# Hybrid Hawk/S5 trunk: four plain pairs of w_up for both halves of the tokens, and a norm plan that makes the plain operands first

## The chip, the cores and the metric

The kernel runs on one core of a Trainium2 chip. Its engines are TensorE (PE; its weight loads are shown apart as PEld), VectorE (DVE), ScalarE (ACT), GpSimd (POOL) and SyncE (SP), which here issues all DMA. Each takes its instructions in the order in which they were recorded. The metric is device time in microseconds of one execution; less is better.

## The reference, cut to what matters

One layer on 1024 prompt tokens and 8 sequences of 4 sample tokens, 1056 tokens of 1024 features. The two groups share weights and differ in state and in the conditioning vectors. All of it is float32.

```python
u = x * (1 + sc1) + sh1
z = u @ w_in + b_in                      # LRU, gate, S5 and merge inputs
...                                      # RG-LRU branch, S5 branch with weight GLU
gl = gelu(ys) @ w_s5_glu
br_b = gl[..., :D_MODEL] * sigmoid(gl[..., D_MODEL:])
mixed = (sigmoid(m_a) * br_a + sigmoid(m_b) * br_b) @ w_out
x = layer_norm(ALPHA * x + g1 * mixed, ln1_g, ln1_b)
u2 = x * (1 + sc2) + sh2
hf = u2 @ w_ffn_up                       # 1024 -> 2 * 2816
f = (silu(hf[..., :D_FF]) * hf[..., D_FF:]) @ w_ffn_down
x = layer_norm(ALPHA * x + g2 * f, ln2_g, ln2_b)
```

## The kernel before

Tokens lie along the free axis, features on the 128 partitions. Every product is made of three matmuls: each operand is split into a high part (a rounded copy, made by ACT) and a low part (the rest, made by a subtraction on DVE or POOL, `lo_part`, which the profile shows as line 117), and high x high, high x low and low x high are summed in one PSUM bank. A weight tile is 128 outputs by 8 k tiles of 128; `WTile.split` makes its two parts in two halves of four k tiles each, ACT first, then DVE for w_up and POOL for all other weights. `use_w` splits one tile ahead of the one in use; raw tiles are loaded up to three ahead into a ring of three.

From the second GLU pass on, the tokens are four quarters of 264, two *halves* (s = 0: quarters 0 and 1; s = 1: quarters 2 and 3). The stages in order:

1. `glu(0)`, `out_pass(0)`, `glu(1)`, `out_pass(1)`: GLU products and output products of each half. The output products feed the first layer norm's sums.
2. The first norm of a half and the modulated operand `u2` of the up product are not one loop. `norm_plan` lists their operations with an engine, a cost and what each reads and writes; `Plan.emit` places them by a greedy schedule on ticks, and `tick()`, called once for each 24-matmul product, records those that are due. The plan of half 0 is recorded among the products of `glu(1)`, the plan of half 1 among the first up products.
3. The up product, 22 pairs j of weight tiles: tile j (the silu side) and tile 22 + j. The *plain way* costs 96 matmuls for a pair and a half: 2 tiles x 2 quarters x 8 k tiles x 3. The other way treats a pair as a 2x2 block product (k in two halves, quarters as columns) and uses the scheme with seven block products instead of eight: 7 x 4 k tiles x 3 = 84 matmuls, but it needs seven combinations of the weights (`prep`: subtractions on DVE, a copy on ACT, a low part) and eight operands of the tokens (0 to 7, `oper` in `norm_plan`), of which 1, 4, 5 and 7 are the four blocks themselves (b11, b21, b22, b12) and 0, 2, 3 and 6 are differences of them. The plain way uses 1, 4, 5 and 7.
4. The down product over the 22 feature tiles in five pieces of k (`DOWN`), `residual` on DVE, then the second norm.

In the up product before: pairs 0 to 4 go the plain way for half 0 alone, while the operands of half 1 are being made. Then come 22 *units* (`UNITS`): pairs 0 to 4 for half 1 alone, pairs 5 to 21 for both halves. In a unit of one half the low part of five of the seven weight combinations is made by DVE, in a unit of two halves all by POOL (`prep`). Operand 7 exists for half 0 alone and only for the plain way; its place is later the fifth buffer of the ring of weight combinations. The evacuations of a unit (`up_evac`) are ACT copies and tanh, and DVE additions and multiplications, in a chain from product to product. `half_out` writes each finished pair and half to a DRAM tensor, `d_f`.

At the start of down, `residual_scale` (ACT, line 1600) scales the normalised tokens, which had been spilled to `d_x`, for the residual; for quarter 1 the eight tiles stand together just ahead of the first down tile, after a load of 1 MB from `d_x` that is issued in the last unit. Feature tiles are loaded back from `d_f` (`f_load`) among the first down tiles.

Names in the rows: `small_t` holds raw weights, norm buffers and evacuation buffers; `rear_t` the tokens of the four quarters (`M`) and, later, differences; `r_t` the operands and the features; `weights_t` split weights; `ps` PSUM. Line 1170 is every matmul of glu, out and up, 1656 of down; 1364 the modulation, 1430 an operand's high part, 1507 a weight combination's, 230 a weight tile's; 1175, 1185 the GLU evacuation's ACT steps; 1559 the plain way's tanh; 1578, 1584, 1588 a unit's ACT steps.

Of the kernel before, what the change touches and what calls it, by code (L numbers as in the profile page):

```python
# [18 lines left out]
FFT = 22  # L19
# [12 lines left out]
PLAIN = 5  # L32
UNITS = [(j, (1,)) for j in range(PLAIN)] + [(j, (0, 1)) for j in range(PLAIN, FFT)]
# [38 lines left out]
def tile_hawk_s5(ctx: ExitStack, tc: tile.TileContext, io):  # L72
# [197 lines left out]
    for j in range(PLAIN):  # L270
        for m in (j, FFT + j):
            queue("up", io["w_up"][m], m)
# [9 lines left out]
    for i, w in enumerate(seq):  # L282
# [6 lines left out]
        elif not w.plain:  # L289
            w.place = lambda z=1024 * (n_split % 2): (wb, z, z + 2048)  # L290
            n_split += w.key != ("in", 15)
# [1030 lines left out]
    class Plan:  # L1322
# [3 lines left out]
        def __init__(self, us, **share):  # L1326
            self.us, self.share, self.ops, self.wrote, self.read = us, share, [], {}, {}
# [11 lines left out]
        def emit(self, first):  # L1339
# [18 lines left out]
            return first + int(max(end.values()) / self.us) + 1  # L1358
# [14 lines left out]
    def norm_plan(plan, s, rr, tmp):  # L1373
# [31 lines left out]
        bufs = dict(zip(names, tmp))  # L1405
        for c in range(2):
            for op in (sub_, mul):
                for i in range(2):
                    for h in range(2):
                        p.add("V", 0.7, (f"sum{i}", f"r{i}")[op == mul:][:1], (f"x{i}{h}{c}",),  # L1410
                              lambda c=c, i=i, h=h, op=op: normal(c, i, h, op))
# [4 lines left out]
            def mod(i, h, name, c=c):  # L1416

                k = tuple(f"{n}{j}" for n in "tvz" for j in range(2))
                p.add("A", 0.9, (f"x{i}{h}{c}",), (name, *k), lambda: modulated(q0 + i, h, c, bufs[name]))
                if q0 + i == 3:  # L1420
                    p.add("V", 0.8, (f"x{i}{h}{c}",), (name,), lambda: modulated_samples(h, c, bufs[name]))

            def diff(out, x, y):
                p.add("V", 0.7, (x, y), (out,), lambda: tt(V, bufs[out], bufs[x], bufs[y], sub_))

            def oper(e, v, name, c=c):
                o, f = operand(v, s), operand(v, s, FT)
                x = bufs[name]
                p.add("A", 0.65, (name,), (f"o{v}{c}",),
                      lambda: A.activation(o[:, 0, 2 * c:2 * c + 2], x, AF.Copy))  # L1430
                eng, us = {"V": (V, 0.75), "P": (P, 1.35)}[e]
                p.add(e, us, (name, f"o{v}{c}"), (),
                      lambda: lo_part(eng, o[:, 1, 2 * c:2 * c + 2], x, f[:, 0, 2 * c:2 * c + 2]))


            mod(0, 0, "b11")
            mod(1, 0, "b12")
            oper("P", 1, "b11")
            mod(1, 1, "b22")
            if s == 0:  # L1440
                oper("P", 7, "b12")
            mod(0, 1, "b21")
            diff("b11", "b12", "b11")
            diff("b12", "b22", "b12")
            oper("V", 2, "b11")
            oper("P", 5, "b22")
            diff("b11", "b22", "b11")
            oper("P", 3, "b12")
            oper("V", 0, "b11")
            oper("V", 4, "b21")  # L1450
            diff("b21", "b21", "b11")
            oper("P", 6, "b21")
# [8 lines left out]
    tmp1 = tuple(M[0][:, 2 * i:2 * i + 2] for i in range(4))  # L1461
    rr1 = {2: B[:, 4], 3: B[:, 5]}

# [62 lines left out]
    assert plan.emit(2) <= 30  # L1526
# [18 lines left out]
    assert plan.emit(1) <= 4 * PLAIN  # L1545
    for j in range(PLAIN):
        ff = B[:, 2 * (j % 2):2 * (j % 2) + 2]
        for m in (j, FFT + j):
            w = use_w("up", m)
# [312 lines left out]
```

## Time and profile before

| | |
|---|---|
| median of three runs | 1853.21 us (1853.14 to 1854.78) |
| profiled execution's own time | 1857.63 us, span of the core 1855.8 us |
| PE busy | 1731.2 us (93%), 13344 matmuls |
| DVE, ACT, POOL busy | 1200.9, 727.5, 1009.6 us |
| first plan starts (sums of half 0) | 926.5 us |
| plain pairs start, end | 1077.9, 1139.9 us |
| one-half units end, two-half units end | 1222.1, 1568.0 us |

A row of the timeline has the start, the time to the end of the last of the merged instructions, engine, line and tiles; in brackets stands the idle time just before and what ended it. A row of the windows has start and end, length, busy time of each engine with its count of instructions, then TensorE's granted clock, the DMA engines' share and GB/s. A row of grouped instructions has busy time and mean ns of one. A busy PE is not a PE at its peak: matmuls overlap, so the time of a stretch by its count is the better measure.

### The profile page before, as it was taken

Reading aid. Unit: us, or ns where it says so; the run is one execution under the profiler, and the core shown is the slowest. Engines: PE = TensorE matmul, PEld = TensorE weight load, DVE = VectorE, ACT = ScalarE, POOL = GpSimd, SP = SyncE. Lnnn points to the kernel's source line nnn. Section 1 sums busy time; section 2 is a strip of 40 time slices with the busy share of each in tenths; the row PEclk is TensorE's granted clock in tenths of the full one; section 3 lists DMA queues with packets and bytes.
Section 4 is the critical chain, followed back from the end, with each engine's and each line's share of the span. In section 5 each row is a group of like instructions: output and inputs, shape, how many; then the busy total and the mean of one; then the engine's idle time right before and its main releaser. Section 6 shows DMA issues by size and latency. Waiting matters only on the chain. (4 is left out here: it accounts for less than half of the span.)

```text
span 1855.8 us, 33890 instructions
## 1 busy us (share of the span) xinstructions
PE 1731.2 (93%) x13344; PEld 1689.3 (91%) x13344; DVE 1200.9 (65%) x1998; ACT 727.5 (39%) x1465; POOL 1009.6 (54%) x829
## 2 busy tenths in 40 slices
PE   6899999999788799999998998799999999999996
PEld 5889889999788799999998997699999999999996
DVE  6889999738878843322776588755545554543587
ACT  4433333335564543222354354334433333111234
POOL 3466657435666642345667723367677775322654
PEclk9999999999989899999999999999999999999998
DMA  9335544441111149675344333224223325932202
GB/s 346 103 102 148 154 137 136 141 133 44 60 52 39 48 126 245 213 241 195 112 148 150 121 100 119 101 86 149 93 93 122 110 93 196 381 125 78 80 31 65
DMA packets 118927, 241.98 MB, mean 130 GB/s; under 512 B 23152, under 2 KB 62320, under 8 KB 115696
## 3 DMA queue, kind: packets, MB, share of 16 engines
q1 hardware_dynamic: 118768, 239.81, 39.6%
q8 instruction: 105, 1.72, 0.4%
q14 instruction: 54, 0.44, 0.1%
HBM read 180.64 MB, written 54.97 MB: 127 GB/s over the span
## 5 line engine op out<-in xcount | busy, mean ns | idle before, releaser
L1170 PE MATMUL ps<-r_t,weights_t 128*128 128x264 f32 x5424 | 681.4, 286 | 26.9 <-DVE small_t L117 15.5
L1170 PEld LDWEIGHTS ps<-r_t,weights_t 128*128 128x128 f32 x5424 | 669.0, 189 | 34.7 <-DVE small_t L117 17.2
L117 POOL TENSOR_TENSOR weights_t<-small_t,weights_t 128x512 fp32r<-128x512 f32 (+3 forms) x292 | 368.7, 1278 | 422.9 <-ACT weights_t L230 333.3
L338 PE MATMUL ps<-r_t,weights_t 128*128 128x352 f32 x3384 | 572.4, 329 | 1.9 <-ACT weights_t L230 1.1
L338 PEld LDWEIGHTS ps<-r_t,weights_t 128*128 128x128 f32 x3384 | 554.6, 193 | 12.3 <-issue 7.9
L230 ACT ACTIVATE weights_t<-small_t 128x512 fp32r<-128x512 f32 (+3 forms) x274 | 144.5, 570 | 232.0 <-PE ps L1656 96.8
L126 DVE SCALAR_TENSOR_TENSOR rear_t<-ps,small_t,rear_t 128x264 f32<-128x264 f32 (+1 forms) x192 | 92.6, 482 | 124.1 <-PE ps L1656 102.5
L1656 PE MATMUL ps<-r_t,weights_t 128*128 128x264 f32 x1344 | 166.9, 286 | 4.9 <-ACT weights_t L230 4.9
L1656 PEld LDWEIGHTS ps<-r_t,weights_t 128*128 128x128 f32 x1344 | 165.7, 190 | 6.1 <-ACT weights_t L230 5.3
L117 DVE TENSOR_TENSOR small_t<-ps,small_t 128x264 f32<-128x264 f32 (+1 forms) x243 | 91.2, 382 | 105.9 <-ACT small_t L1578 75.8
L126 DVE SCALAR_TENSOR_TENSOR rear_t<-rear_t,ps 128x264 f32<-128x264 f32 (+1 forms) x75 | 33.6, 457 | 172.4 <-PE ps L1170 96.3
L117 DVE TENSOR_TENSOR s_t<-s_t 128x128 f32<-128x128 f32 (+3 forms) x200 | 134.4, 720 | 12.0 <-ACT s_t L747 6.3
L117 POOL TENSOR_TENSOR r_t<-rear_t,r_t 128x264 fp32r<-128x264 f32 (+2 forms) x76 | 95.2, 1256 | 74.2 <-ACT r_t L1185 28.5
L117 POOL TENSOR_TENSOR rear_t<-rear_t,small_t 128x264 f32<-128x264 f32 (+1 forms) x109 | 93.1, 876 | 66.0 <-ACT small_t L1233 44.3
L117 POOL TENSOR_TENSOR weights_t<-rear_t,weights_t 128x512 fp32r<-128x512 f32 x64 | 84.1, 1317 | 70.4 <-ACT weights_t L1507 68.0
L117 DVE TENSOR_TENSOR rear_t<-rear_t,small_t 128x32 f32<-128x32 f32 (+3 forms) x139 | 97.1, 707 | 38.7 <-POOL weights_t L117 28.4
L117 POOL TENSOR_TENSOR r_t<-small_t,r_t 128x528 fp32r<-128x528 f32 (+1 forms) x59 | 80.7, 1377 | 39.9 <-ACT r_t L209 26.3
L126 DVE SCALAR_TENSOR_TENSOR lru_t<-lru_t 128x1056 f32<-128x1056 f32 (+1 forms) x52 | 82.0, 1576 | 29.8 <-ACT lru_t L1008 16.4
L1656 PE MATMUL ps<-r_t 128*128 128x264 f32 x768 | 96.7, 286 | 0.8 <-POOL r_t L117 0.8
L1656 PEld LDWEIGHTS ps<-r_t 128*128 128x128 f32 x768 | 94.6, 188 | 1.7 <-POOL r_t L117 1.2
L126 DVE SCALAR_TENSOR_TENSOR lru_t<-lru_t,small_t 128x352 f32<-128x352 f32 (+2 forms) x96 | 87.9, 916 | 3.4
L1170 PE MATMUL ps<-r_t 128*128 128x264 f32 x636 | 83.4, 286 | 4.5 <-DVE small_t L117 4.5
(225 smaller groups left out, 1986.0 us busy)
## 6 DMA issues: line engine op xcount, KB each, us to landing
d_f<-r_t SPq DMA_DIRECT2D x44, 528.0 KB
r_t<-d_f SPq DMA_DIRECT2D x22, 1056.0 KB
small_t<-in_w_up_dram SPq DMA_DIRECT2D x43, 512.0 KB
small_t<-in_w_in_dram SPq DMA_DIRECT2D x40, 512.0 KB
small_t<-in_w_ada_dram SPq DMA_DIRECT2D x32, 512.0 KB
small_t<-in_w_glu_dram SPq DMA_DIRECT2D x32, 512.0 KB
ada_w_t<-in_w_ada_dram SPq DMA_DIRECT2D x16, 512.0 KB
small_t<-in_w_out_dram SPq DMA_DIRECT2D x16, 512.0 KB
```

The source lines that it names most:

```text
L117: e.tensor_tensor(out, a, b, op=op)
L126: e.scalar_tensor_tensor(out, a, s, b, op0=op0, op1=op1)
L230: A.activation(self.hi[:, s], self.raw[:, s], AF.Copy)
L338: PE.matmul(out[:, :NB], a[:, k, :], x[:, h, nb, k, :], start=bool(first and n == 0 and q == 0), stop=bool(last and n == len(kts) - 1 and ...
L1170: PE.matmul(out[:, :Q], a[:, k, :], x(h, k), start=bool(first and n == 0 and q == 0), stop=bool(last and n == len(kts) - 1 and q == 2), sk ...
L1656: PE.matmul(b[:, :Q], a[:, n, :], f[:, h, Q * q:Q * q + Q], start=n == i == 0, stop=k == k1 - 1 and i == 2)
```

## The change

`PLAIN` is four, and the plain loop runs twice, for half 0 and then for half 1; the 18 units that are left have both halves. For half 1 the plain way needs its own operand 7: `b12_in` makes it from the kept block b12, in the place of half 0's operand 7, when the loop changes halves, by two ACT copies and two DVE subtractions. The matmuls of a plain product take k tiles 4 to 7 ahead of 0 to 3, and the quarters' operands are asked for so that operand 7 comes last. Weight tiles of the second plain half are loaded again, and their low parts are made by POOL.

In `norm_plan` the four blocks and their operands come first and the differences after them. Half 0's plan has four buffers for the blocks as before, so each of the two pieces of k (c) is done whole; half 1's plan has eight (all of quarters 0 and 1, spilled by then), so that the blocks of both pieces go ahead of all differences. The plan for half 1 has to place plain operands within the first half's products, the rest within both.

`residual_scale` of quarter 1 goes tile by tile into the first eight down tiles; loads and scalings of the other quarters start one pair earlier than before (pairs 6 and 8, not 7 and 9).

```diff
-PLAIN = 5
-UNITS = [(j, (1,)) for j in range(PLAIN)] + [(j, (0, 1)) for j in range(PLAIN, FFT)]
+PLAIN = 4
+UNITS = [(j, (0, 1)) for j in range(PLAIN, FFT)]
...
-            self.e = V if key[0] == "up" else P
+            self.e = V if key[0] == "up" and key[1][0] == 0 else P
...
-    for j in range(PLAIN):
-        for m in (j, FFT + j):
-            queue("up", io["w_up"][m], m)
+    for s in range(2):
+        for j in range(PLAIN):
+            for m in (j, FFT + j):
+                queue("up", io["w_up"][m], (s, m))
...
+            mod(c, 0, 0, "b11")
+            mod(c, 1, 0, "b12")
+            oper(c, "P", 1, "b11")
+            mod(c, 0, 1, "b21")
+            mod(c, 1, 1, "b22")
             if s == 0:
-                oper("P", 7, "b12")
...
+                oper(c, "P", 7, "b12")
+            oper(c, "V", 4, "b21")
+            oper(c, "P", 5, "b22")
+
+        def differences(c):
+
+            diff(c, "b11", "b12", "b11")
+            oper(c, "V", 2, "b11")
+            diff(c, "b11", "b22", "b11")
+            diff(c, "b22", "b22", "b12")
+            oper(c, "V", 0, "b11")
+            oper(c, "P", 3, "b22")
+            diff(c, "b21", "b21", "b11")
+            oper(c, "P", 6, "b21")
+
+        if two:
+            blocks_of(0)
+            blocks_of(1)
+            differences(0)
+            differences(1)
+        else:
+            for c in range(2):
+                blocks_of(c)
+                differences(c)
...
+    def b12_in(c):
+        o, f = operand(7, 0), operand(7, 0, FT)
+        A.activation(o[:, 0, 2 * c:2 * c + 2], b12_1[c], AF.Copy)
+        lo_part(V, o[:, 1, 2 * c:2 * c + 2], b12_1[c], f[:, 0, 2 * c:2 * c + 2])
+
+    for s in range(2):
+        for j in range(PLAIN):
+            o = 2 * ((PLAIN * s + j) % 2)
+            ff = B[:, o:o + 2]
+            last = s and j == PLAIN - 1
+            for m in (j, FFT + j):
+                if s and m == 0:
+                    b12_in(0)
+                    b12_in(1)
+                w = use_w("up", (s, m))
...
+                    at_ = ((1, s), (4, s)), ((7, 0), (5, s))
+                    mmq(b, w, lambda h, k: operand(*at_[i][k // 4])[:, h, k % 4, :], (4, 5, 6, 7, 0, 1, 2, 3))
...
-    for k in range(8):
-        residual_scale(1, k)
...
             if m < len(F_LOADS[c]):
                 f_load(F_LOADS[c][m])
+            if c == 0:
+                residual_scale(1, m)
```

How the order moves, in three places. First DVE among the products of `glu(1)`, from the last subtractions of the mean for half 0's first piece on. Rows with 128x528 are the plan's; those of line 126 are the GLU evacuation; `r_t<-` is the low part of an operand, `rear_t<-rear_t,ps` the subtraction of a mean, `rear_t<-rear_t,small_t` a multiplication by the inverse root (the last row of the change alone is a difference), `small_t<-` a difference. Before:

```order
L117 TENSOR_TENSOR rear_t<-rear_t,ps 128x528 x2
L117 TENSOR_TENSOR rear_t<-rear_t,small_t 128x528
L117 TENSOR_TENSOR small_t<-rear_t,small_t 128x528
L117 TENSOR_TENSOR r_t<-small_t,r_t 128x528
L117 TENSOR_TENSOR small_t<-rear_t,small_t 128x528
L126 SCALAR_TENSOR_TENSOR rear_t<-rear_t,ps 128x264
L126 SCALAR_TENSOR_TENSOR rear_t<-rear_t 128x264 x2
L117 TENSOR_TENSOR r_t<-small_t,r_t 128x528
L117 TENSOR_TENSOR small_t<-small_t 128x528
```

The change:

```order
L117 TENSOR_TENSOR rear_t<-rear_t,ps 128x528 x2
L117 TENSOR_TENSOR rear_t<-rear_t,small_t 128x528
L117 TENSOR_TENSOR r_t<-small_t,r_t 128x528
L117 TENSOR_TENSOR rear_t<-rear_t,small_t 128x528
L117 TENSOR_TENSOR r_t<-small_t,r_t 128x528
L126 SCALAR_TENSOR_TENSOR rear_t<-rear_t,ps 128x264
L126 SCALAR_TENSOR_TENSOR rear_t<-rear_t 128x264 x2
L117 TENSOR_TENSOR small_t<-rear_t,small_t 128x528
L117 TENSOR_TENSOR rear_t<-rear_t,small_t 128x528
```

Two low parts stand now where the difference `small_t<-rear_t,small_t` stood, ahead of the GLU evacuation, and that difference comes after it.

Second ACT where the plain loop changes halves, in the change alone. Line 1432 is an operand's high part, 209 the high part of a finished pair, 1599 the tanh, 1576 `b12_in`:

```order
L1599 ACTIVATE small_t<-ps 128x264
L1432 ACTIVATE r_t<-rear_t 128x528
L1599 ACTIVATE small_t<-ps 128x264
L230 ACTIVATE weights_t<-small_t 128x512 x2
L1432 ACTIVATE r_t<-rear_t 128x528 x5
L1576 ACTIVATE r_t<-rear_t 128x528 x2
L230 ACTIVATE weights_t<-small_t 128x512 x2
L209 ACTIVATE r_t<-small_t 128x528
```

The copies of operand 7 come behind the last five operand copies of the plan, and ahead of the split of the second tile of the new half.

Third ACT at the start of down; rows of 128x128 are splits of the first down tiles, two for a tile. Before:

```order
L230 ACTIVATE weights_t<-small_t 128x128 x2
L1600 ACTIVATE rear_t<-rear_t,small_t 128x264 x8
L230 ACTIVATE weights_t<-small_t 128x128 x2
L209 ACTIVATE r_t<-small_t 128x528
L209 ACTIVATE r_t<-rear_t 128x528
```

The change:

```order
L230 ACTIVATE weights_t<-small_t 128x128 x4
L1640 ACTIVATE rear_t<-rear_t,small_t 128x264
L209 ACTIVATE r_t<-small_t 128x528
L209 ACTIVATE r_t<-rear_t 128x528
L230 ACTIVATE weights_t<-small_t 128x128 x2
L1640 ACTIVATE rear_t<-rear_t,small_t 128x264
```

The second tile's split now stands ahead of the first scaling, and one scaling follows each later split.

More of the change, by code (lines that the diff above doesn't have):

```diff
@@ L1326, in __init__ @@
         def __init__(self, us, **share):
-            self.us, self.share, self.ops, self.wrote, self.read = us, share, [], {}, {}
+            self.us, self.share, self.ops, self.wrote, self.read, self.plain = us, share, [], {}, {}, []
         def add(self, e, us, reads, writes, fn):
@@ L1357, in emit @@
                 later(first + int(t / self.us), fn)
-            return first + int(max(end.values()) / self.us) + 1
+            return first + int(max(end[n] for n in self.plain) / self.us) + 1, first + int(max(end.values()) / self.us) + 1
     def modulated(q, h, c, out):
@@ L1404, in norm_plan, with key, mod, diff @@
         names = ("b11", "b12", "b21", "b22")
-        bufs = dict(zip(names, tmp))
-        for c in range(2):
+        two = len(tmp) > 4
+        bufs = {f"{n}{c}": tmp[4 * (c and two) + i] for c in range(2) for i, n in enumerate(names)}
+        def key(n, c):
+            return n + (str(c) if two else "")
+        def mod(c, i, h, name):
+            out = bufs[name + str(c)]
+            k = () if two and c else tuple(f"{n}{j}" for n in "tvz" for j in range(2))
+            p.add("A", 0.9, (f"x{i}{h}{c}",), (key(name, c), *k), lambda: modulated(q0 + i, h, c, out))
+            if q0 + i == 3:
+                p.add("V", 0.8, (f"x{i}{h}{c}",), (key(name, c),), lambda: modulated_samples(h, c, out))
+        def diff(c, out, x, y):
+            p.add("V", 0.7, (key(x, c), key(y, c)), (key(out, c),),
+                  lambda: tt(V, bufs[out + str(c)], bufs[x + str(c)], bufs[y + str(c)], sub_))
+        def oper(c, e, v, name):
+            o, f = operand(v, s), operand(v, s, FT)
+            x = bufs[name + str(c)]
+            p.add("A", 0.65, (key(name, c),), (f"o{v}{c}",),
+                  lambda: A.activation(o[:, 0, 2 * c:2 * c + 2], x, AF.Copy))
+            eng, us = {"V": (V, 0.75), "P": (P, 1.35)}[e]
+            p.add(e, us, (key(name, c), f"o{v}{c}"), (),
+                  lambda: lo_part(eng, o[:, 1, 2 * c:2 * c + 2], x, f[:, 0, 2 * c:2 * c + 2]))
+            if v in (1, 4, 5):
+                p.plain.append(len(p.ops) - 1)
+        def blocks_of(c):
             for op in (sub_, mul):
@@ L1414, in norm_plan @@
                       lambda c=c: spill(c))
[L1416 to L1436, printed above, removed]
@@ L1525, in tile_hawk_s5 @@
     norm_plan(plan, 0, rr0, tmp0)
-    assert plan.emit(2) <= 30
+    assert max(plan.emit(2)) <= 30
     later(1, x_load, 2, 0, 6)
@@ L1544, in tile_hawk_s5 @@
     norm_plan(plan, 1, rr1, tmp1)
[L1545 to L1549, printed above, removed]
[L1550 to L1565 removed]
+    n1, n2 = plan.emit(1)
+    assert n1 <= 4 * PLAIN and n2 <= 8 * PLAIN - 4
+    def b12_in(c):
[12 more added lines that the diff above has]
+                w = use_w("up", (s, m))
+                if last and m == j:
+                    unit_load(0)
+                    unit_load(1)
+                for i in range(2):
+                    tick()
+                    b = bank()
+                    at_ = ((1, s), (4, s)), ((7, 0), (5, s))
+                    mmq(b, w, lambda h, k: operand(*at_[i][k // 4])[:, h, k % 4, :], (4, 5, 6, 7, 0, 1, 2, 3))
+                    p = ff[:, i]
+                    if m == j:
+                        A.activation(p, b[:, :Q], AF.Tanh, scale=0.5)
+                        stt(V, p, p, 1.0, b[:, :Q], OP.add, OP.mult)
+                    else:
+                        tt(V, p, p, b[:, :Q], OP.mult)
+                    if last and m != j:
+                        prep(i)
+            half_out(j, s, ff)
     prep(2)
```

41 lines of the change are left out of this document (7 added, 34 removed).

## The prediction

> **What bounds the kernel now.** I read the page's engine totals and slices first, then PE's timeline, then the windows of the stages that the diff touches.
>
> ```profile
> span 1855.8 us, 33890 instructions
> PE   6899999999788799999998998799999999999996
> ```
>
> PE is at nine tenths in most slices, so only its holes pay. The diff reaches slices 20 to 22 (the output products, beside the first norm plan), 24 to 25 (the plain pairs and the one-half units) and 33 (start of down). These windows (busy us of PE, PEld, DVE, ACT, POOL, then clock, DMA) are: second GLU pass from the first plan on; plain pairs; five one-half units; seventeen two-half units.
>
> ```profile
> 928.05:1036.86 108.81, 102.59 (x818) 101.30 (x817) 66.20 (x92) 50.68 (x104) 76.95 (x60) 0.98 0.47 154
> 1077.92:1139.87 61.95, 59.34 (x482) 58.48 (x480) 55.68 (x95) 37.83 (x71) 18.47 (x12) 1.00 0.34 112
> 1139.87:1222.10 82.23, 59.80 (x421) 57.49 (x422) 60.77 (x81) 29.49 (x58) 31.84 (x23) 0.92 0.30 101
> 1222.10:1568.00 345.90, 345.90 (x2858) 345.90 (x2857) 174.45 (x305) 134.70 (x277) 246.05 (x186) 1.00 0.32 111
> ```
>
> The last row is the floor: 17 units of 168 matmuls, 2856, in 345.90 us, 0.1211 us each, without a hole. Against it the 480 plain matmuls need 58.1 and took 61.95 (3.8 lost), the 420 of the one-half units need 50.9 and took 82.23 (**31.4 lost**), and the 816 of the GLU window need 98.8 and took 108.81 (**10.0 lost**).
>
> Why the one-half units lose:
>
> ```profile
> 1165.13 1.07 DVE L117 TENSOR_TENSOR weights_t<-rear_t,weights_t 128x512 fp32r<-128x512 f32 x1
> 1171.05 4.44 PE L1170 MATMUL ps<-r_t,weights_t 128*128 128x264 f32 x24 [2.79 <-DVE small_t L117]
> 1181.61 1.07 DVE L117 TENSOR_TENSOR weights_t<-small_t,weights_t 128x512 fp32r<-128x512 f32 x1
> 1186.00 0.69 DVE L117 TENSOR_TENSOR weights_t<-rear_t,weights_t 128x512 fp32r<-128x512 f32 x1 [0.78 <-ACT weights_t L1507]
> 1187.42 1.76 DVE L117 TENSOR_TENSOR weights_t<-small_t,weights_t 128x512 fp32r<-128x512 f32 x1
> 1187.56 3.01 PE L1170 MATMUL ps<-r_t 128*128 128x264 f32 x12 [2.80 <-DVE small_t L117]
> ```
>
> The same step of two neighbouring units lies 16.5 us apart (1165.13 and 1181.61): seven weight combinations and the evacuations in one chain on DVE and ACT, for 84 matmuls worth 10.2 us. Idle of 2.8 us also costs clock: 24 matmuls then take 4.44 us, not 2.9. With two halves the same preparation serves 168 matmuls, 20.3 us.
>
> **The change, part by part.** (1) *Matmuls.* Before: 5x96 plain, 5x84, 17x168 = 3756. After: 4x2x96 + 18x168 = 3792. 36 more at 0.1211: **+4.4**.
>
> (2) *One-half units gone*: **-31.4**. The eighteenth unit is of the kind that ran 345.90 us without a hole. Their low parts, 25 on DVE (5 units of 5), leave it; POOL takes them in two-half units, where it is busy 246.05 of 345.90. Loads of w_up's tiles go from 54 (10 plain, 44 for units) to 52 (16 and 36): nothing, with the DMA share at 0.30 to 0.34 in these windows.
>
> (3) *The first plan, under the GLU products.*
>
> ```profile
> 968.55 1.84 DVE L117 TENSOR_TENSOR small_t<-rear_t,small_t 128x528 f32<-128x528 f32 x1 [3.72 <-POOL r_t L117]
> 977.53 0.42 DVE L126 SCALAR_TENSOR_TENSOR rear_t<-rear_t,ps 128x264 f32<-128x264 f32 x1
> 978.91 0.42 ACT L1185 ACTIVATE r_t<-rear_t 128x264 fp32r<-128x264 f32 x1 [2.17 <-DVE rear_t L126]
> 979.24 1.13 ACT L230 ACTIVATE weights_t<-small_t 128x512 fp32r<-128x512 f32 x2
> 980.68 3.44 POOL L117 TENSOR_TENSOR weights_t<-small_t,weights_t 128x512 fp32r<-128x512 f32 x2
> 979.91 0.51 PE L1170 MATMUL ps<-r_t,weights_t 128*128 128x264 f32 x2 [1.80 <-ACT weights_t L230]
> 982.47 13.47 PE L1170 MATMUL ps<-r_t,weights_t 128*128 128x264 f32 x96 [2.05 <-POOL weights_t L117]
> 989.20 0.71 DVE L117 TENSOR_TENSOR small_t<-small_t 128x528 f32<-128x528 f32 x1 [6.22 <-POOL r_t L117]
> 996.55 11.96 PE L1170 MATMUL ps<-r_t,weights_t 128*128 128x264 f32 x94 [0.61 <-POOL weights_t L117]
> ```
>
> DVE stands 3.72 us at a difference that waits for a POOL low part; the GLU evacuation behind it comes at 977.53, ACT's copy of it at 978.91, and only then the weight split, for which PE idles. In the new order two operand low parts stand where that difference stood, and the differences follow an evacuation: the split then comes up to the 3.72 earlier, and PE waited 1.80 + 2.05 for it (and 96 matmuls at a lowered clock took 13.47, not 11.6). The 6.22 at 989.20 now stands behind two evacuations instead of ahead of them. Left of the 10.0 lost: I take 3, because POOL stays loaded (76.95 of 108.81); bounds 0 and, if POOL alone set it, 10. **-7.0**.
>
> (4) *Plain pairs.* The 3.8 lost go, **-3.8**, and new waits come. Rows for them:
>
> ```profile
> 1086.93 1.30 DVE L117 TENSOR_TENSOR weights_t<-small_t,weights_t 128x512 fp32r<-128x512 f32 x2
> 1088.61 1.80 DVE L1265 RECIPROCAL small_t<-rear_t 128x264 f32<-128x264 f32 x1
> 1106.34 0.74 DVE L117 TENSOR_TENSOR rear_t<-rear_t,small_t 128x32 f32<-128x32 f32 x4
> 1112.22 2.07 DVE L117 TENSOR_TENSOR weights_t<-small_t,weights_t 128x512 fp32r<-128x512 f32 x2
> 1113.75 6.11 PE L1170 MATMUL ps<-r_t,weights_t 128*128 128x264 f32 x48 [0.35 <-DVE weights_t L117]
> 1120.43 1.28 DVE L117 TENSOR_TENSOR weights_t<-small_t,weights_t 128x512 fp32r<-128x512 f32 x2
> 1142.06 0.51 PE L1170 MATMUL ps<-r_t,weights_t 128*128 128x264 f32 x2 [2.19 <-ACT weights_t L1507]
> L117 DVE TENSOR_TENSOR r_t<-rear_t,r_t 128x528 fp32r<-128x528 f32 x6 | 7.1, 1201 | 0.0
> L117 DVE TENSOR_TENSOR rear_t<-rear_t,ps 128x528 f32<-128x528 f32 x8 | 5.4, 696 | 0.0
> L117 DVE TENSOR_TENSOR small_t<-ps,small_t 128x264 f32<-128x264 f32 x24 | 10.3, 431 | 9.1 <-ACT small_t L1578 5.3 <-PE ps L1170 3.6
> L117 POOL TENSOR_TENSOR weights_t<-rear_t,weights_t 128x512 fp32r<-128x512 f32 x10 | 13.2, 1320 | 21.0 <-ACT weights_t L1507 18.6 <-DVE small_t L117 2.4
> ```
>
> *Late weights, first half.* The k order now begins with tiles 4 to 7, so both halves of a weight tile must be split first. The seventh tile's split ended at 1112.22 + 2.07 = 1114.3; PE wants it at 1077.92 + 6 x 48 x 0.1211 = 1112.8: 1.5. The eighth has about 2 us less DVE work ahead of it now (differences come later): 0.2. Below: 0; above: the 3.8 of before.
>
> *The switch of halves.* The new b12 operand (L1576 in the new file) is copied on ACT behind the last five operand copies, which wait for DVE's last differences. DVE's order from 1086.93 to there: 12 weight halves at 0.65 (7.8), 14 normalisings, 8 differences and 6 low parts at 0.70 (19.6), 14 evacuations at 0.43 (6.0), 16 sample pieces at 0.74 for four (3.0), a reciprocal and seven small steps of the inverse root (1.80 + 7 x 0.43 = 4.8): 41.2 us, so 1128.1 if DVE runs alone. Of these, 28 wide ones cost 1.20 instead of 0.70 when POOL works beside them (the first two group rows). POOL worked 18.47 of 61.95, 30%: +4.2, 1132.3; b12's own copy (0.6, by ACT's row at 979.24) and two low parts (0.85 each at 30%) add 2.3: ready at 1134.6. PE ends the first half at 1077.92 + 46.5 + 1.7 = 1126.1, waits there for weights split on POOL (below, 2.0), and reads b12 after 36 more matmuls, 4.4: 1132.5. Wait **2.0**; bounds 0 (DVE alone) and 12 (all 28 slow: 9.8 more). Behind those two ACT copies stands the next tile's weight split.
>
> *POOL splits in the second half, and the first unit.* The nearest rows are PE's waits for POOL weights in the GLU window, 2.05 and 0.61. I take 2.0 at the switch and 0.65 at each of the next two tiles; bounds 0 and 2.8 each (the longest wait above). The first unit's first combination starts after the last-but-one product, 2.9 us ahead, and needs 0.43 + 2 x 0.69 on DVE, 0.6 on ACT and 1.32 on POOL, 3.7 in all and some 0.1 for each hand-over: about 1.3 late; bounds 0 and the 2.19 of the row at 1142.06.
>
> New waits: 1.5 + 0.2 + 2.0 + 2.0 + 1.3 + 1.3 = **+8.3**.
>
> (5) *residual_scale(1) spread over eight down tiles.*
>
> ```profile
> 1570.88 4.09 ACT L1600 ACTIVATE rear_t<-rear_t,small_t 128x264 f32<-128x264 f32 x8 [4.23 <-DMA rear_t<-d_x]
> 1575.22 14.16 PE L1656 MATMUL ps<-r_t,weights_t 128*128 128x264 f32 x96 [4.01 <-ACT weights_t L230]
> 1583.99 0.51 ACT L230 ACTIVATE weights_t<-small_t 128x128 fp32r<-128x128 f32 x2 [3.05 <-DMA small_t<-in_w_down_dram]
> 1589.92 0.51 ACT L230 ACTIVATE weights_t<-small_t 128x128 fp32r<-128x128 f32 x2 [5.42 <-DMA small_t<-in_w_down_dram]
> 1590.28 9.91 PE L1656 MATMUL ps<-r_t,weights_t 128*128 128x264 f32 x74 [0.90 <-ACT weights_t L230]
> 1570.00:1575.00 5.00, 1.21 (x10) 0.99 (x9) 1.47 (x5) 4.12 (x9) 0.00 (x0) 0.82 1.00 416
> 1580.00:1585.00 5.00, 5.00 (x43) 5.00 (x43) 3.42 (x9) 1.13 (x4) 2.11 (x6) 0.99 1.03 357
> 1585.00:1590.00 5.00, 4.38 (x37) 4.17 (x35) 3.85 (x11) 0.08 (x1) 0.26 (x1) 1.00 0.95 349
> ```
>
> The 4.01 wait goes: the second tile's split now precedes the scaling that waits for DMA. What is late next is the DMA: its engines are full through these windows (shares 1.00, 1.03 and 0.95), the issue order on SP is the same, and the weight tile that lands at 1589.92 lies behind the same bytes. PE would start it at 1590.28 as before, having waited at the fifth tile instead. **0**; bounds -4.9 (both waits go) and +1.
>
> **Sum**, against the profiled execution's 1857.63: +4.4 - 31.4 - 3.8 + 8.3 - 7.0 + 0 = -29.5, 1828.1. That execution stands 4.4 above the median 1853.21; the same difference from the median gives **1824**.
>
> **Rivals.** *DVE's debt is larger* (chance 0.12): all 28 wide operations run slow, b12 waits 9.8 longer, and the GLU window keeps its 10.0: 1824 + 9.8 + 7 = 1841. For it: 55.68 of 61.95 on DVE; against: POOL has little to do in the first half. *The down stage gives its 4.9 too* (0.12): 1819; against it the full DMA rows.
>
> *POOL becomes the bound: slower* (0.03). Every low part of the 18 units is on POOL now, 246.05 / 17 = 14.5 us a unit against PE's 20.3. It decides from a factor 1.41 on; at 1.55 each unit takes 22.4, 18 x 2.1 = 38 more: 1862. DVE's own 0.69 and 1.76 in the rows above show that such a factor exists between the two engines; against it, 17 such units ran without a hole.
> [...]
>
> *It does not do what it says* (0.02): the lost time returns at the seam to the two-half units, 1853.
>
> **Numbers.** Forecast 0.71; the others as given. Range for eight in ten: **1813 to 1838**, from the down stage's gain with few new waits to about DVE's whole debt. A measurement here tells 0.2%, 3.7 us, from no change: faster 0.95, same 0.02, slower 0.03.
>
> **What would show it.** A plain stretch of 768 matmuls of 97 to 105 us; PE's waits there naming DVE or POOL weights, and one on b12 just after the switch; no wait over 3 us in the units; the GLU window below 104; a DMA wait in the first down tiles in place of the 4.01. I am wrong if the plain stretch exceeds 115, if holes appear in the two-half units, or if the GLU window stays at 109.

## The result, and the profile after

The changed kernel takes 1830.07 us (median; 1828.24 to 1832.15) beside 1853.49 of the kernel before on the same chip: a ratio of 0.9873, 95% interval 0.9856 to 0.9890, so 20 to 27 us less. The forecast was 1824, the range 1813 to 1838. The profiled execution took 1828.24. Here are its span and PE's busy tenths from the page.

```profile
span 1826.5 us, 33873 instructions
PE   6999999999878889999999998999999999999996
```

Slices 24 and 25, counted from 0, stood at 8 and 7 (plain pairs and one-half units) and stand at 8 and 9. The windows of the changed kernel: second GLU pass from the first plan on; plain pairs; the eighteen units; from the first down product to the end; of that, the first 19.4 us. (Columns as before: busy time of PE, PEld, DVE, ACT, POOL, granted clock, DMA share, GB/s. In the changed kernel line 1174 stands for 1170, 1693 for 1656, 1432 for 1430 and 1189 for 1185; an experiment's own edit moves some by a few lines more.)

```profile
924.70:1029.13 104.43, 101.12 (x819) 99.84 (x818) 69.92 (x92) 50.89 (x104) 78.69 (x60) 1.00 0.48 160
1070.19:1174.08 103.89, 96.81 (x773) 95.31 (x771) 62.75 (x107) 51.21 (x97) 44.75 (x33) 0.98 0.36 119
1174.08:1540.27 366.19, 366.19 (x3022) 366.19 (x3023) 184.25 (x321) 142.91 (x294) 262.10 (x197) 1.00 0.32 110
1540.27:1826.50 286.23, 266.96 (x2142) 263.63 (x2140) 165.61 (x355) 76.81 (x173) 114.86 (x140) 0.98 0.38 137
1540.27:1559.70 19.43, 15.37 (x111) 14.56 (x110) 10.73 (x26) 4.60 (x12) 7.76 (x12) 0.94 1.02 413
```

And from the first down product to the end in the kernel before:

```profile
1568.07:1855.80 287.73, 267.56 (x2142) 264.19 (x2140) 165.64 (x355) 77.38 (x175) 114.96 (x140) 0.97 0.38 136
```

Where the time went, start of stage to start of stage in the two profiles. From the first plan to the first plain product: 149.87 before (1077.92 - 928.05), 145.49 now (1070.19 - 924.70), 4.4 less, all of it in the GLU window. From the first plain product to the first down product: 490.15 and 470.08, **20.1 less**. From there to the end: 287.73 and 286.23, 1.5 less. That is 26.0. The remaining 3.35 of the 29.3 between the two spans lie ahead of the first plan (928.05 against 924.70), where the diff changes nothing; in the profiles below this point lies anywhere from 923.87 to 928.39. The stages behind it repeat far better: the eighteen units took 366.16 to 366.21 us from start to start in all eleven profiles in which they follow the plain pairs. So I read small effects from stages, and set the timed ratios (uncertain by about 0.0015 each, 3 us) beside them.

PE's rows at the waits that are left, in order: GLU pass, seventh plain tile, switch of halves (two), the tile after it, first unit, down.

```profile
977.37 18.35 PE L1174 MATMUL ps<-r_t,weights_t 128*128 128x264 f32 x144 [1.89 <-POOL weights_t L117]
...
1107.82 11.63 PE L1174 MATMUL ps<-r_t,weights_t 128*128 128x264 f32 x94 [2.08 <-DVE weights_t L117]
1119.90 0.51 PE L1174 MATMUL ps<-r_t,weights_t 128*128 128x264 f32 x2 [0.45 <-ACT weights_t L230]
1122.71 7.86 PE L1174 MATMUL ps<-r_t,weights_t 128*128 128x264 f32 x48 [2.30 <-POOL weights_t L117]
1131.74 6.09 PE L1174 MATMUL ps<-r_t,weights_t 128*128 128x264 f32 x48 [1.17 <-POOL weights_t L117]
...
1174.08 11.67 PE L1174 MATMUL ps<-r_t,weights_t 128*128 128x264 f32 x94 [0.83 <-POOL weights_t L117]
...
1556.77 153.94 PE L1693 MATMUL ps<-r_t,weights_t 128*128 128x264 f32 x1248 [3.33 <-ACT weights_t L230]
```

The plain stretch has 768 matmuls, 93.0 us at 0.1211, and took 103.89: 10.9 lost. The wait of 2.30 and the 48 matmuls behind it, 7.86 us in place of some 5.9, are the largest piece. What made the split late at that place, on DVE, ACT and POOL:

```profile
1113.31 3.59 DVE L117 TENSOR_TENSOR r_t<-rear_t,r_t 128x528 fp32r<-128x528 f32 x2
...
1117.16 2.06 DVE L117 TENSOR_TENSOR rear_t<-rear_t 128x528 f32<-128x528 f32 x3
1117.89 0.65 ACT L1432 ACTIVATE r_t<-rear_t 128x528 fp32r<-128x528 f32 x1 [4.43 <-DVE rear_t L117]
...
1118.71 1.14 ACT L230 ACTIVATE weights_t<-small_t 128x512 fp32r<-128x512 f32 x2
...
1119.41 3.25 POOL L117 TENSOR_TENSOR weights_t<-small_t,weights_t 128x512 fp32r<-128x512 f32 x2 [3.08 <-ACT weights_t L230]
```

The row at 1117.16 makes differences. ACT stands 4.43 us at an operand copy that waits for one of them; the weight split (1118.71) is queued behind that copy, and POOL's part (1119.41) behind the split.

### The profile page after: what moved, and what is told of

It is laid out like the page before. It is cut to its first block, busy times and chain, and to the rows that moved or that the text cites. A ratio compares the mean times of both kernels' runs of the same rounds, so it can differ in the third digit from the quotient of the medians.

```text
span 1826.5 us, 33873 instructions
## 1 busy us (share of the span) xinstructions
PE 1726.6 (95%) x13380; PEld 1687.1 (92%) x13380; DVE 1161.9 (64%) x1946; ACT 719.0 (39%) x1448; POOL 1021.5 (56%) x839
## 4 chain that ended last, share of the span: by engine, by line
PE 64%; DVE 14%; POOL 9%; issue 6%; DMA 3%; ACT 2%; SPq 0%; POOLq 0%; DVEq 0%; ACTq 0%
PE ps L1174 36%; PE ps L342 13%; PE ps L1693 12%; DVE s_t L117 7%; POOL weights_t L117 3%; POOL r_t L117 3%; POOL lru_t L117 2%; DVE left_t L117 1%; DVE s_t L774 1%; DVE rear_t L117 1%; DMA ada_w_t<-in_w_ada_dram 1%; PE ps L401 1%; DVE s_t L126 1%; DMA small_t<-in_w_in_dram 1%; PE ps L748 1%
## 5 line engine op out<-in xcount | busy, mean ns | idle before, releaser
L117 POOL TENSOR_TENSOR weights_t<-small_t,weights_t 128x512 fp32r<-128x512 f32 (+3 forms) x312 | 395.5, 1283 | 438.1 <-ACT weights_t L230 358.9
L230 ACT ACTIVATE weights_t<-small_t 128x512 fp32r<-128x512 f32 (+3 forms) x286 | 151.4, 572 | 245.8 <-PE ps L1693 95.3
L117 DVE TENSOR_TENSOR small_t<-ps,small_t 128x264 f32<-128x264 f32 (+1 forms) x228 | 84.8, 379 | 102.4 <-ACT small_t L1618 74.5
L117 POOL TENSOR_TENSOR weights_t<-rear_t,weights_t 128x512 fp32r<-128x512 f32 x57 | 75.2, 1323 | 55.9 <-ACT weights_t L1534 55.9
L126 DVE SCALAR_TENSOR_TENSOR lru_t<-lru_t 128x1056 f32<-128x1056 f32 (+1 forms) x52 | 81.8, 1574 | 29.7 <-ACT lru_t L1012 16.3
L1693 PE MATMUL ps<-r_t 128*128 128x264 f32 x768 | 96.7, 286 | 0.8 <-POOL r_t L117 0.8
L117 POOL TENSOR_TENSOR left_t<-s_t 128x512 f32<-128x512 f32 (+1 forms) x40 | 76.9, 1944 | 5.9 <-DVE s_t L117 3.5
```

Source lines behind the costliest of these rows:

```text
L117: e.tensor_tensor(out, a, b, op=op)
L126: e.scalar_tensor_tensor(out, a, s, b, op0=op0, op1=op1)
L230: A.activation(self.hi[:, s], self.raw[:, s], AF.Copy)
L1693: PE.matmul(b[:, :Q], a[:, n, :], f[:, h, Q * q:Q * q + Q], start=n == i == 0, stop=k == k1 - 1 and i == 2)
```

## The experiments

Ratios are to the kernel before, timed in the same series. The changed kernel was run once more as a control.

> The changed kernel once more, beside the next experiments. Expected on any theory: a ratio of 0.986 to 0.988 against the kernel before.

1832.94 us, ratio 0.9874 (0.9860 to 0.9888): the same.

**One-half units.** Two experiments on the largest term, -31.4. First, two one-half units back:

```diff
-UNITS = [(j, (0, 1)) for j in range(PLAIN, FFT)]
+PLAIN1 = 2
+UNITS = [(j, (1,)) for j in range(PLAIN1, PLAIN)] + [(j, (0, 1)) for j in range(PLAIN, FFT)]
...
-        for j in range(PLAIN):
+        for j in range((PLAIN, PLAIN1)[s]):
```

> The changed kernel, but the second half has two plain pairs; pairs 2 and 3 of it are made by one-half units as before (24 matmuls fewer). Theory: a one-half unit costs 16.5 us where its matmuls are worth 10.2, so two of them cost 12.6 and the 24 matmuls give back 2.9: 9.7 us above the changed kernel, with waits of 2 to 3 us on DVE in the two units. Rival: the loss of the one-half units belonged to the half-1 plan's leftovers, which are done by then: 2.9 us below the changed kernel. Second rival: their lead over PE (four parts prepared ahead) carries the first of the two: some 3 us above.

1837.23 us, ratio 0.9897 (0.9883 to 0.9911). The window from the first plain to the first down product, and a wait in it:

```profile
1070.82:1547.32 476.50, 464.61 (x3770) 462.69 (x3769) 264.81 (x451) 197.58 (x399) 304.58 (x227) 0.99 0.32 110
```

```profile
1158.76 3.01 PE L1175 MATMUL ps<-r_t,weights_t 128*128 128x264 f32 x12 [3.56 <-DVE small_t L118]
```

The same window of the control:

```profile
1071.76:1541.86 470.10, 463.05 (x3794) 461.57 (x3793) 246.85 (x427) 194.27 (x391) 307.06 (x229) 1.00 0.33 112
```

That is 6.4 us more (4.3 between the timed medians, in the same series), with 24 matmuls (2.9) fewer: 9.3 lost in two units, 4.7 each, where the five of the kernel before lost 6.3 each. So the loss comes back with the units; the sign refutes the first rival, and the size lies halfway between the theory's 9.7 and the 3 of a lead that carries the first unit.

Second, the kernel before with its one-half units kept and their low parts moved to POOL:

```diff
-        lo_part(V if len(UNITS[u][1]) == 1 and v % 3 != 2 else P, w.lo, src, rg.v(o, 4, 128))
+        lo_part(P, w.lo, src, rg.v(o, 4, 128))
```

> The kernel before, with all low parts of the one-half units' weight combinations on POOL (before: five of seven on DVE). Theory: the amount of work on DVE sets the pace of the one-half units. A unit took 16.5 us with some 12.2 us of busy DVE; without its five low parts DVE has 6.9 left, POOL goes from 6.4 to about 13 us a unit, and that sets the pace: five units in 62 to 70 us in place of 82.2, time 12 to 20 us below the kernel before. Rival: the chain from the combination to its copy to its low part to the matmul sets the pace, not an engine's load: the window stays at 80 us or more, time within 2 us of before, so that only a second half of tokens for each preparation helps.

1847.65 us, ratio 0.9950 (0.9935 to 0.9964). The window of the five one-half units, and two rows in it:

```profile
1137.17:1210.07 72.90, 56.66 (x420) 54.56 (x421) 40.21 (x56) 29.33 (x58) 63.25 (x48) 0.95 0.33 110
```

```profile
1187.53 0.64 ACT L209 ACTIVATE r_t<-small_t 128x528 fp32r<-128x528 f32 x1 [2.14 <-POOL small_t L117]
...
1189.01 0.43 DVE L117 TENSOR_TENSOR small_t<-ps,small_t 128x264 f32<-128x264 f32 x1 [4.00 <-ACT small_t L1578]
```

82.2 us became 72.9, 9.3 of the 31.4: the rival's 80 is refuted, and the theory's 62 to 70 (12 to 20 us less time) is not reached. The work that a unit's preparation lays on an engine counts: DVE's busy time fell from 60.8 to 40.2, and POOL, now busy for 63.3 of 72.9, took its place. It is not all, since DVE had been busy for only 60.8 of 82.2. ACT waits for POOL's product of a finished pair, DVE's evacuation waits behind ACT, and PE waits for the evacuation, so that the wait still carries DVE's name. Another engine for the low parts gives 9.3 of the 31.4 back; a second half of the tokens for the same preparation gives all of it.

**The plain stretch.** Two edits alone, then both. The k order of the first plain half:

```diff
-                    mmq(b, w, ..., (4, 5, 6, 7, 0, 1, 2, 3))
+                    mmq(b, w, ..., (4, 5, 6, 7, 0, 1, 2, 3) if s else range(8))
```

> The changed kernel, but with the k tiles of the first plain half's matmuls in the order 0 to 7 (the second half keeps 4 to 7 ahead of 0 to 3). Theory: the wait of 2.1 us for the seventh weight tile's second half on DVE goes, since the first product then begins with the part that is split first: plain stretch 103.9 to 102, time 1828. Rival: DVE is behind by a fixed amount, and PE, earlier by 2 us, waits that much longer at the next tile or at the switch of halves: plain stretch 103.9, time 1830.

1828.88 us, ratio 0.9858 (0.9843 to 0.9873). Window of the plain stretch and PE's rows:

```profile
1070.36:1173.90 103.54, 97.33 (x773) 95.44 (x771) 62.76 (x107) 51.08 (x97) 44.42 (x33) 0.98 0.36 119
```

```profile
1106.26 12.25 PE L1174 MATMUL ps<-r_t,weights_t 128*128 128x264 f32 x94 [0.38 <-DVE weights_t L117]
1119.73 0.51 PE L1174 MATMUL ps<-r_t,weights_t 128*128 128x264 f32 x2 [1.22 <-ACT weights_t L230]
1122.54 7.87 PE L1174 MATMUL ps<-r_t,weights_t 128*128 128x264 f32 x48 [2.30 <-POOL weights_t L117]
```

The wait of 2.08 fell to 0.38, and the stretch only from 103.89 to 103.54: the rival is right. PE arrived earlier and waited longer at the switch, which ends when DVE, ACT and POOL end it. Holding the differences back:

```diff
+            p.add("gate", 51, (), ("gate",), lambda: None)
             differences(0)
             differences(1)
...
-            p.add("V", 0.7, (key(x, c), key(y, c)), (key(out, c),),
+            g = ("gate",) if two else ()
+            p.add("V", 0.7, (key(x, c), key(y, c), *g), (key(out, c),),
```

> The changed kernel, with the differences of half 1 and their operands held back until the second plain half has begun (an entry in the plan that ends at 51 us on the plan's clock, read by each difference). Theory: the differences and their operand copies, which stand on DVE and ACT ahead of the first weight splits of the second half, make those splits late: the waits at the switch (0.45, 2.30, 1.17, 0.26 us) and the matmuls at a lowered clock behind them (about 2.0 us) go for the most part; plain stretch 103.9 to 98 to 100 us, time 1825 to 1826. Rival: POOL's splits (3.25 us for two halves) are the price of the switch by themselves: PE still waits 2 us or more for POOL weights there, the plain stretch stays at 102 to 104, time 1829 to 1830. Second rival: the differences only make the same lateness in the second half: waits there, 1830 or more.

1825.44 us, ratio 0.9838 (0.9823 to 0.9853). Window and rows:

```profile
1071.36:1170.61 99.25, 95.77 (x772) 95.11 (x770) 66.46 (x107) 51.57 (x97) 46.55 (x33) 0.98 0.38 124
```

```profile
1108.98 36.71 PE L1174 MATMUL ps<-r_t,weights_t 128*128 128x264 f32 x288 [2.08 <-DVE weights_t L117]
1146.26 23.52 PE L1174 MATMUL ps<-r_t,weights_t 128*128 128x264 f32 x192 [0.57 <-POOL weights_t L117]
```

4.6 us less, and at the switch 288 matmuls run without a wait, though its weights are split on POOL as before. So POOL's splits were not late by themselves; they stood behind the differences. Both edits:

> The changed kernel with both edits of the two experiments on the plain stretch: differences of half 1 held back until the second plain half, and k tiles 0 to 7 in order in the first half. With the differences held back the plain stretch was 99.25 us, of which 2.08 us are the wait for the seventh weight tile and some 1.6 us the matmuls at a lowered clock behind it. Theory: with nothing behind it at the switch that a late DVE would make up, the k order now gives those 3.7 us, which it did not give alone: plain stretch 95.5 to 96.5, 3 to 3.5 us below the kernel with held-back differences and 7.5 to 8 below the changed kernel. Rival: DVE's debt is still there and only shows at the next tile: plain stretch 98 to 99.3.

1823.07 us, ratio 0.9827 (0.9814 to 0.9840).

```profile
1071.58:1167.80 96.22, 94.42 (x772) 93.55 (x771) 68.09 (x107) 51.56 (x97) 47.22 (x33) 1.00 0.39 128
```

The k order, worth 0.35 alone, is worth 3.0 once the differences are out of the way, as the theory had it. Of the 10.9 lost, 3.2 are left.

**The GLU window.** Half 0's plan in the old order, the rest as changed (the edit is the old list of operations, as the diff above has it in its removed lines, for half 0):

> The changed kernel, with the first norm plan (half 0, under the second GLU pass) in the old order. Theory: the new order is what shortened the second GLU pass from 108.8 us to 104.4 us (first plan's start to the last product), so the window is back at 108 to 109 us and the time 4.4 us above the changed kernel's 1830.1: 1834.5. The prediction's own price was 7.0: 1837. Rival: the window differs between the two profiles through its granted clock alone (0.98 and 1.00), not through the order: window 104 to 105 us, time 1830. Second rival: half 1's plan and the plain products want what the new order made ready sooner, so that the plain stretch (103.9 us) grows too.

1835.28 us, ratio 0.9890 (0.9875 to 0.9904).

```profile
927.47:1036.20 108.73, 102.52 (x818) 101.23 (x817) 66.23 (x92) 50.67 (x104) 76.95 (x60) 0.98 0.47 154
```

The window is back at 108.7, and from the first plan to the first plain product it takes 149.90, as before the change; the plain stretch stays at 103.85. DVE's wait of 3.72 for a POOL low part and PE's waits of 1.80 and 2.05 are back with it. So the order gave the 4.4; every profile with the new order and no other edit in this window has 145.5 to 146.05 there. For the 5.6 that are left (104.43 less 98.8), these rows of the changed kernel stand ahead of its longest wait there, the 1.89 at 977.37:

```profile
967.05 2.55 DVE L126 SCALAR_TENSOR_TENSOR rear_t<-rear_t 128x264 f32<-128x264 f32 x2
...
969.52 1.80 DVE L117 TENSOR_TENSOR small_t<-rear_t,small_t 128x528 f32<-128x528 f32 x1
...
971.43 1.08 DVE L117 TENSOR_TENSOR rear_t<-rear_t,small_t 128x528 f32<-128x528 f32 x1
972.43 0.42 DVE L126 SCALAR_TENSOR_TENSOR rear_t<-rear_t,ps 128x264 f32<-128x264 f32 x1
...
973.81 0.43 ACT L1189 ACTIVATE r_t<-rear_t 128x264 fp32r<-128x264 f32 x1 [1.81 <-DVE rear_t L126]
974.14 1.13 ACT L230 ACTIVATE weights_t<-small_t 128x512 fp32r<-128x512 f32 x2
...
975.59 3.45 POOL L117 TENSOR_TENSOR weights_t<-small_t,weights_t 128x512 fp32r<-128x512 f32 x2
```

Wide DVE operations ahead of the evacuation at 972.43, ACT's copy waiting for it, the split behind that, and POOL's two halves, 3.45 us. Two attempts, one for POOL and one for DVE. In the first, DVE makes one half of each weight tile's low part:

```diff
-                lo_part(self.e, self.lo[:, s], self.raw[:, s], hf[:, s])
+                e = V if self.key[0] == "glu" and self.key[1][0] == 1 and s.start else self.e
+                lo_part(e, self.lo[:, s], self.raw[:, s], hf[:, s])
```

> The changed kernel, but in the second GLU pass the second half of each weight tile's low part is made by DVE and not by POOL. Theory: what is left of the loss in that window (5.6 us, PE waiting for POOL weights) comes from POOL's queue, two halves of 1.3 to 1.7 us behind the plan's low parts: with one of them on DVE the waits on POOL shrink, window 104.4 to 101 or 102 us, time 2 to 3 us below the changed kernel. Rival: DVE is as loaded there (69.9 of 104.4 us, its wide operations lengthened beside POOL), so the wait only changes its name to DVE: window 104 to 107, time the same or up to 3 us more.

1835.83 us, ratio 0.9901 (0.9884 to 0.9917).

```profile
926.65:1037.10 110.45, 103.39 (x819) 101.57 (x818) 78.06 (x106) 50.69 (x104) 57.36 (x46) 0.98 0.45 149
```

POOL has 21 us less to do there, DVE 8 more, and the window is 6.0 longer: beyond the rival's 3. PE still waits for POOL's halves in five places, 4.4 us together (3.3 in the changed kernel), so it is not the amount of POOL's work that makes them late. What less work on POOL would give without the 8 us on DVE is not shown. The other attempt, on top of the best kernel below, spread the plan thinner:

```diff
-    plan = Plan(2.9, V=0.5, A=0.5, P=0.5)
+    plan = Plan(2.9, V=0.45, A=0.5, P=0.45)
```

> The kernel with held-back differences, the k order 0 to 7 and the later loads, and a first norm plan that is spread thinner: its clock grants DVE and POOL 0.45 of their time in place of 0.5, so that it ends two products later. Theory: what is left of the loss in the second GLU pass (104.4 us in place of 98.8) is the plan's wide DVE operations standing in clusters ahead of the evacuations; thinner clusters make the evacuation, and with it the weight splits, less late: window 102 to 103 us, first plan's sums to the plain products 145.5 to 144 us, time 1.5 us below the kernel without this edit. Rival: the work on DVE and POOL is the same, each waits for the other as long, and the waits only move: 104 to 106 us, time within 1.5 us of it, or above.

1819.56 us, ratio 0.9808 (0.9794 to 0.9821).

```profile
923.87:1031.03 107.16, 103.48 (x819) 102.44 (x817) 65.88 (x92) 53.78 (x106) 75.71 (x60) 0.97 0.47 156
```

2.7 longer than the 104.4 of the kernel without this edit, and beyond the rival's 106; the timed ratios (0.9808, and 0.9805 without it) cannot tell the two apart. What sets the last 5.6 us is open; these two runs only say that neither moving POOL's work to DVE nor a lower density of the plan is the handle.

**Down.** The scalings of quarter 1 together ahead of the first down tile again:

```diff
     lag[0] = 2
+    for k in range(8):
+        residual_scale(1, k)
...
-            if c == 0:
-                residual_scale(1, m)
```

> The changed kernel, with the eight residual scalings of quarter 1 together ahead of the first down tile, as before. Theory: the bytes in the DMA queue set the first down tiles, so PE only waits at another tile: from the start of down to the end 286.2 us becomes 287.8 at most, the wait at the second down tile is back at about 4 us, the one at the fifth tile falls from 3.3 to about 1 us; time 1830.1 to 1831.7. Rival: the wait of 4 us came from the scalings standing ahead of the weight split, and spreading them gave it all: 1834 to 1835, both waits in the trace.

1830.01 us, ratio 0.9861 (0.9844 to 0.9877). From the first down product to the end, and PE's two waits:

```profile
1541.92:1829.90 287.98, 267.18 (x2142) 263.72 (x2140) 164.94 (x355) 77.39 (x175) 114.80 (x140) 0.98 0.39 136
```

```profile
1549.87 13.83 PE L1696 MATMUL ps<-r_t,weights_t 128*128 128x264 f32 x96 [4.79 <-ACT weights_t L230]
1564.48 149.64 PE L1696 MATMUL ps<-r_t,weights_t 128*128 128x264 f32 x1224 [0.78 <-ACT weights_t L230]
```

The large wait is back at the second tile (4.79) and the one after the fifth is 0.78; the stage is 1.2 to 1.8 longer than in the two profiles of the changed kernel (286.74 and 286.23). The timed runs do not show it: their ratio is some 2 us the other way, within the uncertainty. Now the bytes: feature tiles loaded later.

```diff
-    F_LOADS = (range(5, 13), range(13, 18), (18, 19, 20), (21,))
+    F_LOADS = ((None,) * 4 + (5, 6, 7, 8), range(9, 17), (17, 18, 19, 20), (21,))
```

> The changed kernel, with the feature tiles 5 to 21 loaded back later: none beside the first four down tiles, 5 to 8 beside the other four, 9 to 16 in the second piece of k, 17 to 20 in the third (before: 5 to 12 beside the first eight down tiles). Each load is about 1.08 MB. Theory: the bytes ahead of the weight tiles in the DMA queue set PE's wait of 3.3 us at the fifth down tile (and the 0.7 at the third), and that is why spreading the residual scalings gave so little: with four loads fewer in front (4.3 MB, some 10 us at 413 GB/s) the waits go, from the start of down to the end 286.2 us becomes 282 to 283, time 3.5 to 4 us below the changed kernel. Rival: the weight tiles are issued late, when a raw buffer comes free, and not behind other bytes: the wait stays, time within 1 us of the changed kernel. Second rival: the later loads miss their use in the third piece: new waits, slower.

1827.75 us, ratio 0.9853 (0.9839 to 0.9868). Windows (its first 19.5 us of down, then all of it) and PE's row at the fifth tile:

```profile
1542.91:1562.40 19.49, 18.29 (x141) 17.32 (x140) 13.14 (x34) 6.72 (x18) 9.57 (x16) 1.00 0.90 343
1542.91:1824.60 281.69, 265.35 (x2142) 262.12 (x2140) 165.23 (x355) 77.32 (x173) 115.17 (x140) 0.98 0.40 139
```

```profile
1556.78 152.03 PE L1693 MATMUL ps<-r_t,weights_t 128*128 128x264 f32 x1248 [0.77 <-ACT weights_t L230]
```

3.33 became 0.77, the stage 281.69: 4.5 to 5.1 less than in the two profiles of the change, the DMA share at 0.90 where it was 1.02. Some 2.6 of it are the wait, and 1.9 are the 1248 matmuls behind it (152.03, where they took 153.94). The fifth tile's load on the chain that ended last, in the changed kernel and here (start, time to landing):

```profile
1546.11 10.20 DMA small_t<-in_w_down_dram
1548.41 7.90 DMA small_t<-in_w_down_dram
```

It landed in 7.90 us in place of 10.20, so the weight tile had lain behind the feature tiles' bytes. It is also issued late, as the rival has it, though the hold is not a raw buffer: 5.8 and 5.5 us after the first down product, because SP issues it behind the store of a finished pair. That store waits for POOL's low part, and POOL for ACT's copy, which stands behind the first of the scalings; this one waits 3.02 us for `d_x` in the changed kernel. No run here takes that part away. With both edits of the plain stretch:

> The kernel with held-back differences and the k order 0 to 7 in the first plain half, and the later loads of the feature tiles. Theory: the gains lie in different stages and add: plain stretch 96.2 us, from the start of down to the end 282 to 283, time 3.5 us below the 1823.1 of the one without the later loads, ratio to the kernel before 0.981. Rival: an earlier end of the up product leaves the down stage waiting longer for its bytes: 1822 to 1823.

**1818.41 us, ratio 0.9805 (0.9791 to 0.9820)**: the gains add. This is the fastest kernel here, some 13 us faster than the change (0.9805 against 0.9874 of 1855). The plain stretch is 96.22 us again; from the first down product to the end:

```profile
1536.29:1818.80 282.51, 265.41 (x2142) 262.07 (x2140) 165.47 (x355) 77.33 (x173) 115.21 (x140) 0.98 0.40 139
```

## Why the prediction was right, and where its sizes were off

The sum was -29.5; the stages that the diff reaches gave -26.0, the timed medians -23.4. The first plan and the plain pairs each came out 2.6 short of their terms, and the 1.5 that down gave, which had stood at 0, made up for part of that by luck. By its steps:

1. *Matmuls, +4.4*, and 2. *one-half units, -31.4*: right. The eighteen units took 366.19 us for 3024 matmuls, 0.1211 each, without a hole. The reason, preparation that serves too few matmuls, held: moved to POOL it loads POOL in DVE's place, and two units brought back cost 4.7 us each. That is less than the 6.3 that the term used, and 16.5 us is not the pace of every unit: by PE's matmuls the five before took about 18.5, 16.9, 16.5, 15.4 and 14.9 us, and the two brought back 16.3 and 13.9. The first of those had a wait of 0.23 us ahead of it where there had been 2.19; the last in each case stands beside two-half units, whose low parts are POOL's. Whether that is all of the difference is not shown.

3. *The first plan, -7.0*: **mis-sized; -4.4**. The mechanism (DVE's wait for a POOL low part ahead of the evacuation) is the right one, since the old order brings all 4.4 back, with the waits named. The step that failed is "the split then comes up to the 3.72 earlier", and with it "left of the 10.0 lost: I take 3": counted from the plan's start the split comes 1.75 earlier (974.14 - 924.70 against 979.24 - 928.05), and 5.6 are left. These are the windows from the same step of DVE to the evacuation, before (964.83 to 977.53) and now:

```profile
964.83:977.53 12.70, 12.70 (x107) 12.70 (x106) 8.85 (x9) 5.45 (x12) 10.92 (x8) 1.00 0.39 126
961.48:972.43 10.95, 10.74 (x89) 10.53 (x88) 10.04 (x10) 4.45 (x10) 10.46 (x7) 1.00 0.24 66
```

The wait is gone, but DVE's busy time (the third of the five) rose from 8.85 to 10.04: the operations that took the place of the wait take long here, among them one difference of 1.80 us that still stands ahead of the evacuation. The reason given for the 3, that "POOL stays loaded", was not borne out: with 21 us less on POOL, and 8 more on DVE, the window grew.

4. *Plain pairs, -3.8 and +8.3*: the old waits went, the new ones cost **10.9**. The single waits were near: 2.08 for the seventh tile (predicted 1.5), 2.30 for POOL weights at the switch (2.0), 1.17 and 0.26 at the next two tiles (1.3), 0.83 at the first unit (1.3); b12 shows 0.93 and 0.36 in the control's profile (2.0), and nothing in the other, where POOL's wait covers it. Two things failed. The list left out the clock granted behind a wait, some 2 us of slow matmuls behind the 2.30 (7.86 for 48, at a granted clock of 0.65 and then 0.88). And it added up waits that are not separate: nearly all are DVE's one debt. Taking the first of them away alone gave 0.35, taking the differences away gave 4.6, and then the first gave 3.0. The POOL term rested on POOL's slowness (the waits of the GLU window), and POOL was on time once the differences were gone. The debt itself was sized a little low: DVE had operand 7 ready 59.1 us into the stretch, where the count gave 56.7. One reading in that count was wrong: its second group row (696 ns) is the subtraction of the mean, which reads PSUM, so the two rows do not show one operation with POOL beside it and without. In the changed kernel, from 1070 to 1132 us, that form took 696 ns again, and the 128x528 forms with both inputs in SBUF took 1074 to 1125 on average. The timelines of DVE and POOL do show DVE taking longer beside POOL: in the plain pairs of the kernel before, the 128x528 operations with both inputs in SBUF took 0.69 to 0.71 us where no POOL operation ran at the same time (13 of them) and 1.28 on average, up to 1.83, where one did (9); those that read PSUM took 0.69 to 0.70 in both cases (6 and 2).

5. *residual_scale, 0*: -1.5 in the stage, within its bounds (-4.9 to +1), and the place of the new wait, the fifth tile, was right. The full DMA (a share of 1.02 in the first 19.4 us) was the cause of most of it, as the later loads show. The rival "down gives its 4.9 too" was wrong for this change, but 4.5 us are there for one that moves bytes.

Of the signs named, the plain stretch (103.9, predicted 97 to 105), the names of its waits, the units without holes and the DMA wait in down came; the GLU window missed its mark of 104 by 0.4. POOL as the bound did not come: 262.10 us for eighteen units are 14.6 a unit, against 20.3 on PE.

## What to carry to other kernels

Where an engine prepares operands for PE, first count how many matmuls one preparation serves; here serving a second half of the data was worth 31.4 us, and moving part of the preparation to another engine 9.3. Do not add up waits that stem from one late engine: remove the work that makes it late (here, differences that nobody needs yet), and only then polish the single waits. When DMA is full (here a share of 1.02), look for large loads that are not needed yet ahead of small ones that are due; moving them was worth 4.5 to 5.1 us here.

## What the runs showed of the hardware that was not expected

The same wait of 2.08 us at the seventh plain tile was followed by a full clock in one profile of the changed kernel (the row at 1107.82: 94 matmuls in 11.63, at a granted clock of 1.00) and by a lowered one in the other, the control:

```profile
1109.35 13.45 PE L1174 MATMUL ps<-r_t,weights_t 128*128 128x264 f32 x96 [2.08 <-DVE weights_t L117]
...
1129.56 0.39 PE L1174 MATMUL ps<-r_t,weights_t 128*128 128x264 f32 x1 [0.93 <-ACT r_t L1576]
```

```profile
1109.35:1111.35 2.00, 2.00 (x13) 2.00 (x14) 1.93 (x7) 1.40 (x3) 0.00 (x0) 0.76 0.51 123
1111.35:1113.35 2.00, 2.00 (x11) 2.00 (x11) 1.45 (x7) 2.00 (x5) 0.00 (x0) 0.50 0.36 143
1113.35:1115.35 2.00, 2.00 (x16) 2.00 (x16) 2.00 (x5) 1.64 (x4) 1.10 (x1) 0.89 0.00 0
```

Behind the idle of 2.08 the granted clock was 0.76, 0.50 and 0.89 in these three stretches of 2 us, and the 96 matmuls took 1.6 us more. Both plain stretches ended after 103.89 us all the same: where the clock fell early, PE waited less at the switch (1.46 us, where the other profile has 0.45 and 2.30). Of the seven profiles with this wait of 2.08, two ran on at full pace (94 matmuls in 11.63 and, in `e9_late_f`, 11.64); in the control, `e1_old_plan0`, `e2_scale_ahead` and `e7_two_half_units` the next 96 took 13.43 to 13.45, and in `e4_late_diff` the granted clock was 0.83, 0.50 and 0.82 in the three stretches of about 2 us behind it. What decides between the two is not shown.
